# Output projection weights: split at the attention's end, or split on the way and kept in DRAM

## The chip, the cores and the metric

The kernel runs on one core of a Trainium2 chip. Its time is the device time of one launch in microseconds (us). Three runs of the kernel before took 2853.21, 2858.51 and 2867.74 us; the median is 2858.51. One further execution was taken with the hardware profiler; all views below are of that one.

## The reference, cut to what matters

Two transformer layers of width 1024 over 1024 prompt positions (one sequence) and 128 sample positions (8 streams of 16). Both groups go through the same layers, the sample group with cached keys and values.

```python
for l in range(2):
    sh_m, sc_m, g_m, sh_f, sc_f, g_f = split(silu(c) @ w_ada[l] + b_ada[l], 6)   # adaLN
    h = x * (1 + sc_m) + sh_m
    if l == 0:      # 16 query heads on 4 key/value heads of 64, own chunk of 64 + 2 back, sinks
        q, k, v = split(h @ w_qkv_a)
        o = band_attend(q, k, v, t5_bias, sinks, n_back=2);   mix = o @ w_o_a
    else:           # 16 heads, own chunk + 8 back; k, v projected once from x after layer 0
        q = h @ w_q_b
        o = band_attend(q, k_b, v_b, relclip_bias, None, n_back=8);  mix = o @ w_o_b
    x = layer_norm(ALPHA * x + (1 + g_m) * mix, ...)
    f = conv_ffn(x * (1 + sc_f) + sh_f, w_up[l], conv_w[l], conv_b[l], w_down[l])  # GEGLU, width 2816
    x = layer_norm(ALPHA * x + (1 + g_f) * f, ...)
# band_attend: s = q k^T * 64**-0.5 + bias, masked to the band; softmax (layer 0 with sink); p v
```

`o @ w_o_a` and `o @ w_o_b` are the output projections: 1024 x 1024 weights, 4 MB in fp32 each.

## The kernel before, in words

**High and low parts.** Wide products are made of fp32r matmuls on values split in two: a high part (the fp32 value cast to fp32r) and a low part (value minus high part). A product takes three matmuls: low by high, high by low, high by high. `split` (L174) does the cast on ACT (`copy`, L165) and the subtraction on POOL or DVE (L176). `wload` (L178) brings a piece of weights: SP issues the load of 128 x 1024 fp32 (512 KB) into `ws`, a staging ring of two buffers, and `split` writes its parts into a pair of buffers:

```python
s = (ring or self.ws).next()
self.nc.sync.dma_start(s, src)
h, l = dst or self.wring.next()
self.split(s, h, l, eh, el)
```

**Attention** (`attention`, L374). 16 heads (8 head pairs `c`, two heads `a` each) by 4 pairs of 128-row query tiles give 64 steps. A step issues, in this order: the scores of its pair (`scores`, L518: matmuls L546 with the high and L549 with the low part of the keys; bias, row minimum and exponential from L512 on), what the table `QAT` puts there of the query projection, the transposes of an earlier pair's probabilities (`weigh`, L557: matmul L572, high part L577 on ACT, low part L578 on DVE), and that pair's product with the values (`values`, L581: matmul L591, copy L602 on ACT, add L603 on DVE). After every second pair of a head, `normalise` (L621) multiplies by the reciprocal sums, which go to DRAM (rD) and come back spread over 64 rows (L628).

The query projection of head pair c is one `wload` (`qload`) and three blocks of 24 matmuls (`qblock`; the matmuls have line L302). Its weights go into `wslots[0:2]`, two slots, each a pair of `wh` and `wl` buffers of 128 x 1024:

```python
QAT[8 * c] = [(c + 1, None)]          # load weights of pair c + 1
self.wring = Ring(self.wslots[0:2])
```

The sample positions are 16 items, issued at the steps in `ITEMS` (matmuls and copies L672 to L735; one of them is the transpose L700). Layer 0's attention also carries the adaLN products of later use (`ada`, L237: matmuls of 32 x 256 with weights loaded into one buffer of `F`), a piece per step. Outputs `on` of head pairs 0 to 6 go to DRAM (`oN`) and are loaded and split into `H` at the steps in `OAT` (`oload`, L634); pair 7's are split from `on` itself.

During an attention, `wslots[2]` and half of `wslots[3]` hold split probabilities, the other half of `wslots[3]` holds keys, and `X1` (in the views `x1att`) holds keys, values and queries.

**Output projection** (`out_proj`, L921). Eight `wload`s bring the weights into eight pairs of buffers, all of them free again only as the attention ends: `wslots[0:2]`, parts of `X1`, `wslots[2]`. The first four are subtracted on POOL, the last four on DVE:

```python
w = [self.wload(wo[i // 4, i % 4], el="ppppvvvv"[i], dst=d) for i, d in enumerate(loc)]
```

`ln_gate` loads the gate row spread over 128 partitions into `gateP` = F[2048:3072]; `on` lies in F[2176:3200]. For each tile of 128 positions and half of the columns, `half` makes 24 matmuls (`mmX`, L314), multiplies by the gate (L948) and adds the residual (L949). Tile 8, the sample positions, comes third; its input is loaded from DRAM (`oSD`) and split (L966, L165, L176).

**What sets the order.** All transfers are issued by SP, one after the other. The program runs in a tile framework that orders each engine's instructions with its own model of time; instructions marked with `issue_after` follow a named one. Names in the views are of buffers (PS: the 8 banks of TensorE's results; HX: the buffer that holds `H`; C: small constants and sums; gatt: `rb`, `olo` and sample values of the attention).

Of the kernel before, what the change touches and what calls it, by code (L numbers as in the profile page):

```python
# [35 lines left out]
for c in range(5):  # L36
    QAT[8 * c] = [(c + 1, None)]
    for j, k in enumerate((1, 3, 6)):
        QAT[8 * c + k] = [(c + 1, j)]
QAT.update({40: [(6, None)], 41: [(6, 0)], 43: [(6, 1)], 46: [(6, 2)], 48: [(7, None), (7, 0)], 49: [(7, 1)], 50: [(7, 2)]})  # L40
OAT = {51: (0, 1), 52: (2,), 53: (3,), 54: (4,), 55: (5,), 61: (6,)}
ITEMS = [24 + 3 * k for k in range(8)] + [51 + (3 * k) // 2 for k in range(8)]
# [51 lines left out]
class Trunk:  # L94
    def __init__(self, ctx, tc, I, O):
# [4 lines left out]
        nc = self.nc  # L100
# [40 lines left out]
        self.vH = [dr.tile([1024, R[l] // 64, 128], F32, name=f"vH{l}") for l in range(2)]  # L141
        self.vS = [dr.tile([128, R[l]], F32, name=f"vS{l}") for l in range(2)]
        self.oN = dr.tile([7, 128, 1024], F32, name="oN")
        self.actD = dr.tile([NFF, 128, TOK], F32, name="actD")
# [229 lines left out]
    def attention(self, l, wk):  # L374
# [77 lines left out]

        self.wring = Ring(self.wslots[0:2])
        sbt = []
# [24 lines left out]
        def qblock(c, bi, w):  # L479
# [13 lines left out]
            for a in range(2):  # L493
                r = slice(64 * a, 64 * a + 64)
                o = slice(64 - 64 * a, 128 - 64 * a)
                hi = qs(c, a, r, s0, m)
                src = self.tiles(ps[r, 0:m])
                nc.scalar.activation(hi, src, AF.Copy, scale=-SCALE)
                nc.vector.scalar_tensor_tensor(
                    qs(c, a, o, s0, m), src, -SCALE, hi.bitcast(F32), op0=ALU.mult, op1=ALU.subtract  # L500
                )

        qw = {}
# [130 lines left out]
        def oload(c):  # L634
            s = self.ws.next()
            nc.sync.dma_start(s, self.oN[c])
            self.split(self.tiles(s), self.Hx(0, c, 0, 1024), self.Hx(1, c, 0, 1024), "a", "p")
# [130 lines left out]
        for i, x in enumerate(work):  # L768
# [19 lines left out]
            for c in OAT.get(i, ()):  # L788
                oload(c)
        assert not items  # L790
        for f in steps:
# [129 lines left out]
    def out_proj(self, l, xsrc, xdst, aff):  # L921
        nc, I, H = self.nc, self.I, self.H
        wo = I[("wo0", "wo1")[l]]
        X1 = self.X1
        loc = ((5120, 6144), (7168, 8192), (0, 2048), (3072, 1024))
        loc = [tuple(X1[:, o : o + 1024] for o in p) for p in loc]
        loc = self.wslots[0:2] + loc + [self.wslots[2], (X1[:, 4096:5120], self.wslots[3][1])]
        w = [self.wload(wo[i // 4, i % 4], el="ppppvvvv"[i], dst=d) for i, d in enumerate(loc)]
        w0, w1 = w[0:4], w[4:8]
        F = self.F  # L930
# [606 lines left out]
```

## Time and profile before

| what | value |
|---|---|
| runs | 2853.21, 2858.51, 2867.74 us, median 2858.51 |
| profiled execution | 2860.57 us, its span 2858.7 us |
| mean granted TensorE clock | 0.978 of full speed |
| PE busy | 2728.7 us, 95% of the span |
| DVE busy | 1675.0 us, 59% |
| ACT busy | 1404.6 us, 49% |
| POOL busy | 1078.0 us, 38% |
| transfers | 454.48 MB, mean 159 GB/s |

PE is TensorE's matmuls, PEld its weight loads, DVE VectorE, ACT ScalarE, POOL GpSimd, SP SyncE, which issues the transfers. A table by stretches gives for each the length, the busy time of PE, PEld, DVE, ACT and POOL with the number of instructions, the granted clock (1.00 is 2.4 GHz, 0.50 is 1.2 GHz), the mean busy share of the 16 DMA engines and what they moved in GB/s. A time line gives start, duration, engine, line, operation, output <- inputs, shape, and in brackets how long the engine had been idle and whose end it then started after. The scores of layer 0's attention begin at 112 us, those of layer 1's at 1589 us; the attentions end near 430 and 1975 us.

### The profile page before, as it was taken

The numbers are of one execution on the slowest core, as the hardware profiler recorded it, in microseconds if no ns is written. First come the engines' busy times: TensorE is split into PE (matmuls) and PEld (weight loads), VectorE is DVE, ScalarE is ACT, GpSimd is POOL, SyncE is SP. The second block draws the span as 40 slices with busy tenths as digits, with TensorE's granted clock in tenths as the row PEclk, the third lists the DMA queues.
The fourth block names the chain that finished last, engine by engine and source line by source line (L and its number), as shares of the span: only waits on it lengthen the run. The fifth ranks groups of instructions, "written<-read, shape, count | busy, mean of one in ns | idle before, by whom it ended". The sixth has DMA issues, their size and how long they took to land.

```text
span 2858.7 us, 48892 instructions
## 1 busy us (share of the span) xinstructions
PE 2728.7 (95%) x18086; PEld 2434.9 (85%) x18086; DVE 1675.0 (59%) x3841; ACT 1404.6 (49%) x2990; POOL 1078.0 (38%) x1104
## 2 busy tenths in 40 slices
PE   7999889899999999999999999988999999999998
PEld 4987767899999998788999888866799999997886
DVE  4365656765454556665412677774866555566764
ACT  3464643554444444445424676663465545554441
POOL 2122335776565640000550121231877666640000
PEclk9999989999999999999999999999999999999999
DMA  8655433244444448766785467683232222238662
GB/s 314 179 149 170 114 120 111 91 132 136 153 136 150 133 142 289 246 200 230 257 289 165 125 156 179 171 257 108 89 96 79 70 78 80 77 111 274 224 202 77
DMA packets 215199, 454.48 MB, mean 159 GB/s; under 512 B 38992, under 2 KB 114976, under 8 KB 214576
## 3 DMA queue, kind: packets, MB, share of 16 engines
q1 hardware_dynamic: 214960, 451.35, 49.7%
q8 instruction: 143, 2.34, 0.3%
q14 instruction: 96, 0.79, 0.1%
HBM read 359.40 MB, written 101.30 MB: 161 GB/s over the span
## 4 chain that ended last, share of the span: by engine, by line
PE 68%; issue 6%; DMA 4%; DVE 4%; ACT 2%; POOL 1%; SPq 0%; POOLq 0%; DVEq 0%; ACTq 0%
PE PS L1098 33%; PE PS L1249 15%; PE PS L302 7%; PE PS L314 7%; PE PS L591 1%; DMA ws<-in_wdn_dram 1%; PE PS L237 1%; PE PS L572 1%; DVE F L512 1%; PE PS L546 1%; PE PS L883 1%; DMA ws<-in_wo_dram 1%; PE PS L549 1%; DVE HX L176 0%; DMA F<-gd 0%
## 5 line engine op out<-in xcount | busy, mean ns | idle before, releaser
L176 POOL TENSOR_TENSOR wl<-ws,wh 128x512 fp32r<-128x512 f32 (+1 forms) x219 | 329.5, 1508 | 669.0 <-ACT wh L165 600.2
L1152 DVE SCALAR_TENSOR_TENSOR PS<-F,PS 128x512 f32<-128x512 f32 (+2 forms) x704 | 348.0, 515 | 141.0 <-ACT PS L1159 60.1
L1098 PE MATMUL PS<-HX,wh 128*128 128x288 f32 x2616 | 402.8, 298 | 14.1 <-DVE F L948 11.3
L165 ACT CAST wh<-ws 128x512 fp32r<-128x512 f32 (+1 forms) x321 | 244.9, 768 | 331.3 <-PE PS L1249 98.6
L1098 PEld LDWEIGHTS PS<-HX,wh 128*128 128x128 f32 x2616 | 366.0, 190 | 22.8 <-DVE F L948 11.7
L1249 PE MATMUL PS<-wh,HX 128*128 128x512 f32 x1164 | 364.6, 392 | 7.6 <-DVE HX L176 7.6
L1249 PEld LDWEIGHTS PS<-wh,HX 128*128 128x128 f32 x1164 | 219.5, 189 | 53.8 <-DVE HX L176 8.5
L1098 PE MATMUL PS<-HX,wl 128*128 128x288 f32 x1536 | 253.8, 296 | 1.0 <-DVE F L1134 0.7
L302 PE MATMUL PS<-HX,wh 128*128 128x384 f32 x1248 | 247.6, 340 | 0.0
L1249 PE MATMUL PS<-wl,HX 128*128 128x512 f32 x582 | 227.8, 391 | 0.6 <-DVE wl L176 0.6
L1098 PEld LDWEIGHTS PS<-HX,wl 128*128 128x128 f32 x1536 | 219.9, 188 | 7.6 <-issue 7.1
L302 PEld LDWEIGHTS PS<-HX,wh 128*128 128x128 f32 x1248 | 218.3, 190 | 4.6 <-issue 3.1
L314 PE MATMUL PS<-wh,HX 128*128 128x256 f32 (+1 forms) x936 | 173.7, 316 | 16.0 <-ACT wh L165 7.3
L1098 PE MATMUL PS<-x1att,wh 128*128 128x288 f32 x1168 | 182.2, 297 | 0.5 <-DVE x1att L176 0.5
L1159 ACT ACTIVATE PS<-F 128x512 f32<-128x512 f32 x176 | 138.2, 785 | 74.8 <-DVE F L1131 61.9
L165 ACT CAST HX<-F 128x384 fp32r<-128x384 f32 (+3 forms) x232 | 135.3, 602 | 75.5 <-PE PS L1249 15.6
L628 POOL TENSOR_TENSOR F<-F,gatt 64x512 f32<-64x512 f32 x62 | 79.4, 1281 | 243.9 <-DVE F L603 201.9
L176 DVE TENSOR_TENSOR HX<-F,HX 128x384 fp32r<-128x384 f32 (+3 forms) x204 | 147.2, 733 | 40.8 <-ACT HX L165 37.9
L1098 PEld LDWEIGHTS PS<-x1att,wh 128*128 128x128 f32 x1168 | 163.9, 188 | 5.9 <-issue 4.9
L314 PEld LDWEIGHTS PS<-wh,HX 128*128 128x128 f32 x936 | 137.5, 195 | 27.4 <-ACT wh L165 7.7
L1249 PE MATMUL PS<-HX 128*128 128x512 f32 x630 | 147.7, 394 | 4.5 <-ACT HX L165 4.5
L302 PE MATMUL PS<-HX,wl 128*128 128x384 f32 x624 | 133.4, 351 | 12.9 <-DVE HX L167 7.2
(242 smaller groups left out, 5515.4 us busy)
## 6 DMA issues: line engine op xcount, KB each, us to landing
F<-in_adaw_dram SPq DMA_DIRECT2D x106, 512.0 KB
ws<-in_wup_dram SPq DMA_DIRECT2D x92, 512.0 KB
ws<-in_wdn_dram SPq DMA_DIRECT2D x88, 512.0 KB
actD<-F SPq DMA_DIRECT2D x44, 576.0 KB
F<-actD SPq DMA_DIRECT2D x132, 192.0 KB
F<-in_wdn_dram SPq DMA_DIRECT2D x44, 512.0 KB
x1att<-kH SPq DMA_DIRECT2D x60, 256.0 KB
xd<-F SPq DMA_DIRECT2D x27, 512.0 KB
```

What stands on the lines that cost most here:

```text
L165: self.lastact = nc.scalar.copy(out, in_).ins
L176: self.eng(el).tensor_sub(lo, src, hi.bitcast(F32))
L237: mm = nc.tensor.matmul(ps[32 * j : 32 * j + 32, hf * 256 : hf * 256 + 256], self.cT[:, k * 32 : k * 32 + 32], w[n][:, j * 256 : j * 256 + ...
L302: self.nc.tensor.matmul(out, w[a][:, k * 128 : k * 128 + 128], self.Hx(p, k, s0, n), start=i == 0, stop=i == 23)
L314: self.nc.tensor.matmul(out[:, 0:n], H[:, t0 // 128, p, j * kn + k, :], w[a][:, k * n : k * n + n], start=i == 0, stop=i == 23,)
L512: nc.vector.tensor_tensor_reduce(out=p[:, c0 : c0 + w], in0=ps, in1=b, scale=1.0, scalar=init, op0=ALU.add, op1=ALU.min, accum_out=nm)
L546: mm = nc.tensor.matmul(o, q, khi[a][:, kc], start=first, stop=False, **kw)
L628: self.eng("v" if last else "p").tensor_mul(on[r, q], on[r, q], rb[r, :])
L1098: nc.tensor.matmul(out, w[f][a][:, k * 128 : k * 128 + 128], x[:, k, :], start=start and i == 0, stop=i == 11, skip_group_check=True,)
L1152: nc.vector.scalar_tensor_tensor(o, v, w(i), o, op0=ALU.mult, op1=ALU.add)
L1159: nc.scalar.activation(yp, u[:, bl, 2:258], AF.Identity, bias=w(3), scale=w(2))
L1249: nc.tensor.matmul(ps, h[p][:, i * 128 : i * 128 + 128], w[q][:, hf * 512 : hf * 512 + 512], start=j == 0 and k == 0, stop=j == NFF - 1 an ...
```

## The change

A new table, `WAT`, puts one function call at the end of steps 3, 9, 15, ..., 45 of each attention. The call, `wpre(i)`, does a `wload` of piece i of the output weights into `wslots[1]` (cast on ACT, subtraction on POOL) and stores both parts to `woD`, a new DRAM tensor. The query weights use `wslots[0]` alone. `out_proj` loads the 16 parts from `woD` into the same buffers as before and does no cast and no subtraction.

```diff
+WAT = {3 + 6 * i: i for i in range(8)}
...
+        self.woD = [dr.tile([8, 2, 128, 1024], F32, name=f"woD{l}") for l in range(2)]
...
-        self.wring = Ring(self.wslots[0:2])
+        self.wring = Ring(self.wslots[0:1])
...
+        def wpre(i):
+            w = self.wload(I[("wo0", "wo1")[l]][i // 4, i % 4], dst=self.wslots[1])
+            for p in range(2):
+                nc.sync.dma_start(self.woD[l][i, p], w[p].bitcast(F32))
...
             for c in OAT.get(i, ()):
                 oload(c)
+            if i in WAT:
+                wpre(WAT[i])
...
-        wo = I[("wo0", "wo1")[l]]
...
-        w = [self.wload(wo[i // 4, i % 4], el="ppppvvvv"[i], dst=d) for i, d in enumerate(loc)]
-        w0, w1 = w[0:4], w[4:8]
+        for i, d in enumerate(loc):
+            for p in range(2):
+                nc.sync.dma_start(d[p].bitcast(F32), self.woD[l][i, p])
+        w0, w1 = loc[0:4], loc[4:8]
```

The lines below a changed place move: L165, L176, L237 and L302 of before are L167, L178, L239 and L304 in the changed kernel, L546, L549, L572, L578, L591, L603 and L628 are L553, L556, L579, L585, L598, L610 and L635, and L948 is L958.

What stands on DVE at the end of layer 0's attention, from the last-but-one add L603 to the first product with the gate L948. L578 makes the last low parts of probabilities, `HX<-F,HX` of 128x1024 is the split of oSD, `HX<-F,HX` of 128x4x128 that of one half of pair 7's outputs, `wl<-ws` a split of output weights. Before:

```order
L176 TENSOR_TENSOR x1att_309<-ws,x1att_309 128x1024
L603 TENSOR_TENSOR F<-PS,gatt_310 64x256
L578 TENSOR_TENSOR wh<-PS,wh 128x512
L176 TENSOR_TENSOR HX<-F,HX 128x4x128
L176 TENSOR_TENSOR HX<-F,HX 128x1024
L603 TENSOR_TENSOR F<-PS,gatt_310 64x256 x2
L628 TENSOR_TENSOR F<-F,gatt_310 64x512
L176 TENSOR_TENSOR wl<-ws,wh 128x1024
L176 TENSOR_TENSOR wl<-ws,x1att_309 128x1024
L176 TENSOR_TENSOR HX<-F,HX 128x4x128
L948 TENSOR_TENSOR F<-PS,F 128x512 x2
```

The same place in the changed kernel:

```order
L610 TENSOR_TENSOR F<-PS,gatt_312 64x256
L585 TENSOR_TENSOR wh<-PS,wh 128x512
L610 TENSOR_TENSOR F<-PS,gatt_312 64x256
L178 TENSOR_TENSOR HX<-F,HX 128x4x128
L610 TENSOR_TENSOR F<-PS,gatt_312 64x256
L635 TENSOR_TENSOR F<-F,gatt_312 64x512
L178 TENSOR_TENSOR HX<-F,HX 128x1024
L178 TENSOR_TENSOR HX<-F,HX 128x4x128
L958 TENSOR_TENSOR F<-PS,F 128x512 x2
```

The subtractions of weights are gone, and the split of oSD stands behind the last adds and the last product with the reciprocal sums.

DVE at the end of layer 1's attention, with the same names. Before:

```order
L603 TENSOR_TENSOR F<-PS,gatt_12281 64x256
L578 TENSOR_TENSOR wh<-PS,wh 128x512
L578 TENSOR_TENSOR wh<-PS,wh 128x256
L176 TENSOR_TENSOR HX<-F,HX 128x1024
L176 TENSOR_TENSOR wl<-ws,wh 128x1024
L603 TENSOR_TENSOR F<-PS,gatt_12281 64x256
L176 TENSOR_TENSOR wl<-ws,x1att_12280 128x1024
L628 TENSOR_TENSOR F<-F,gatt_12281 64x512
L176 TENSOR_TENSOR HX<-F,HX 128x4x128
```

And in the changed kernel:

```order
L610 TENSOR_TENSOR F<-PS,gatt_12315 64x256
L585 TENSOR_TENSOR wh<-PS,wh 128x512
L178 TENSOR_TENSOR HX<-F,HX 128x1024
L585 TENSOR_TENSOR wh<-PS,wh 128x256
L610 TENSOR_TENSOR F<-PS,gatt_12315 64x256
L635 TENSOR_TENSOR F<-F,gatt_12315 64x512
L178 TENSOR_TENSOR HX<-F,HX 128x4x128
L958 TENSOR_TENSOR F<-PS,F 128x512 x2
```

Here the last low part of probabilities (128x256) stands behind the split of oSD instead of ahead of it.

PE at the start of layer 0's attention, where the projection of head pair 1 begins (L302, `PS<-HX,wl` first) behind that of pair 0. Before, with 4 attention matmuls and 4 of adaLN between the two projections:

```order
L302 MATMUL PS<-HX,wh 128x384 x16
L546 MATMUL PS<-x1att_309 128x128
L549 MATMUL PS<-x1att_309 128x128
L546 MATMUL PS<-x1att_309 128x256
L549 MATMUL PS<-x1att_309 128x256
L237 MATMUL PS<-F,C 32x256 x4
L302 MATMUL PS<-HX,wl 128x384 x8
```

In the changed kernel, the last rows of what stands between them:

```order
L579 MATMUL PS<-C,F 128x128 x2
L553 MATMUL PS<-x1att_311 128x256
L556 MATMUL PS<-x1att_311 128x256
L239 MATMUL PS<-F,C 32x256 x4
L553 MATMUL PS<-x1att_311 128x256
L556 MATMUL PS<-wl,x1att_311 128x256
L304 MATMUL PS<-HX,wl 128x384 x8
```

There the scores of more steps and the first transposes of probabilities (L579) come ahead of pair 1's projection, 19 score matmuls and transposes in all.

## Rows read from the trace of the kernel before

**Rows 1.** The page, busy us of each engine, share of the span, instructions.
```profile
PE 2728.7 (95%) x18086; PEld 2434.9 (85%) x18086; DVE 1675.0 (59%) x3841; ACT 1404.6 (49%) x2990; POOL 1078.0 (38%) x1104
```

**Rows 2.** Table by stretches, layer 0: us, engines, clock, DMA share, GB/s.
```profile
140.00:180.00 40.00, 39.67 (x296) 35.74 (x296) 26.38 (x90) 27.60 (x86) 10.74 (x14) 1.00 0.52 161
...
340.00:360.00 20.00, 14.31 (x99) 10.30 (x98) 13.09 (x56) 13.74 (x45) 8.62 (x9) 0.73 0.44 116
360.00:380.00 20.00, 18.12 (x130) 13.48 (x131) 13.29 (x52) 12.06 (x34) 9.73 (x6) 0.67 0.33 100
...
400.00:420.00 20.00, 17.72 (x104) 13.09 (x103) 7.04 (x17) 5.21 (x8) 6.64 (x4) 0.83 0.36 113
420.00:440.00 20.00, 13.10 (x45) 9.88 (x45) 8.68 (x12) 6.10 (x8) 3.82 (x3) 0.78 0.48 152
```

**Rows 3.** Table by stretches, layer 1.
```profile
1740.00:1780.00 40.00, 39.17 (x330) 33.49 (x330) 30.61 (x102) 27.05 (x70) 8.09 (x9) 1.00 0.80 213
...
1880.00:1900.00 20.00, 17.33 (x166) 13.38 (x164) 15.23 (x55) 11.72 (x30) 5.44 (x6) 0.97 1.02 286
```

**Rows 4.** Time line of ACT, end of layer 0: start, us, work, idle before.
```profile
406.75 1.05 ACT L165 CAST x1att<-ws 128x1024 fp32r<-128x1024 f32 x1 [5.13 <-DMA ws<-in_wo_dram]
...
413.76 1.05 ACT L165 CAST x1att<-ws 128x1024 fp32r<-128x1024 f32 x1 [4.96 <-DMA ws<-in_wo_dram]
...
422.23 1.04 ACT L165 CAST HX<-F 128x1024 fp32r<-128x1024 f32 x1 [3.64 <-DMA F<-oSD]
```

**Rows 5.** Time line of PE, end of layer 0.
```profile
409.96 0.44 PE L700 MATMUL PS<-C,F 128*128 128x128 f32 x2 [1.38 <-DVE HX L578]
...
425.03 1.54 PE L591 MATMUL PS<-wh,x1att 128*128 128x256 f32 x6 [2.94 <-DVE F L603]
427.98 2.08 PE L314 MATMUL PS<-wh,HX 128*128 128x512 f32 x4 [1.40 <-ACT wh L165]
```

**Rows 6.** Time line of DVE, end of layer 0.
```profile
427.46 0.69 DVE L628 TENSOR_TENSOR F<-F,gatt 64x512 f32<-64x512 f32 x1
428.19 1.23 DVE L176 TENSOR_TENSOR wl<-ws,wh 128x1024 fp32r<-128x1024 f32 x1
...
430.46 0.68 DVE L176 TENSOR_TENSOR HX<-F,HX 128x512 fp32r<-128x512 f32 x1
437.03 1.29 DVE L948 TENSOR_TENSOR F<-PS,F 128x512 f32<-128x512 f32 x2 [5.88 <-DMA F<-gd]
```

**Rows 7.** Time line of PE, end of layer 1.
```profile
1898.14 0.55 PE L572 MATMUL PS<-C,F 128*128 128x128 f32 x3 [1.97 <-DVE wh L578]
...
1909.22 1.02 PE L572 MATMUL PS<-C,F 128*128 128x128 f32 x6 [1.28 <-DVE wh L578]
...
1919.24 0.97 PE L572 MATMUL PS<-C,F 128*128 128x128 f32 x5 [1.35 <-DVE HX L578]
...
1932.34 0.72 PE L314 MATMUL PS<-wh,HX 128*128 128x512 f32 x2 [2.10 <-DVE C L512]
```

**Rows 8.** Time line of ACT, end of layer 1.
```profile
1867.24 1.05 ACT L165 CAST HX<-ws 128x1024 fp32r<-128x1024 f32 x1 [1.30 <-DMA ws<-oN]
...
1896.32 1.04 ACT L165 CAST wh<-ws 128x1024 fp32r<-128x1024 f32 x1 [2.72 <-DMA ws<-in_wo_dram]
```

**Rows 9.** Time line of DVE, end of layer 1.
```profile
1967.23 1.23 DVE L176 TENSOR_TENSOR wl<-ws,x1att 128x1024 fp32r<-128x1024 f32 x1
```

**Rows 10.** Time line of ACT, start of layer 0's attention.
```profile
113.81 1.04 ACT L165 CAST wh<-ws 128x1024 fp32r<-128x1024 f32 x1
```

**Rows 11.** Time line of POOL, start of layer 0's attention.
```profile
114.93 2.40 POOL L176 TENSOR_TENSOR wl<-ws,wh 128x1024 fp32r<-128x1024 f32 x1 [32.96 <-ACT wh L165]
```

**Rows 12.** Waits of PE, 100 to 340 us: total us, times, longest.
```profile
PE PS L237 <- DMA F<-in_adaw_dram: 5.8, 8, 2.7
```

**Rows 13.** The chain that ended last: start, us, what.
```profile
410.25 3.49 DMA ws<-in_wo_dram
...
1376.36 5.32 DMA hmD<-F
```

## The prediction

> **What bounds the kernel now.** I read the page's busy shares first, then the table by stretches over the two attentions, then the time lines of PE, ACT and DVE where the attentions end, then who waited for whom. PE is busy 95% of the span and no other engine over 59% [rows 1], so PE bounds it and a change is worth what it adds to or takes from PE's idle and slow time. In the middle of an attention there is next to none (39.67 of 40 us busy at a clock of 1.00, row 140:180 of [rows 2]), because the query projections (L302) fill PE between the scores. It lies at the end, where these are used up: PE is idle 5.7, 1.9, 2.3 and 6.9 us in the four 20 us stretches of layer 0's end that [rows 2] show, and the granted clock falls to 0.73, 0.67, 0.83 and 0.78. A granted clock c over a stretch of 20 us between the levels 1.2 and 2.4 GHz means (1 - c) * 2 * 20 us at the lower one: 10.8, 13.2, 6.8 and 8.8 us, 39.6 us together.
>
> The output weights sit in that end. The eight casts stand in ACT's queue among the copies that the attention needs, and ACT stood idle 5.13 and 4.96 us before two of them until their loads had landed [rows 4]. The attention's own copies (L577, L602) were behind. On PE this shows as 1.38 us (released by L578's result), 2.94 us (by L603) and 1.40 us (by a weight cast) of idle time [rows 5]. At the very end DVE's product with the gate (L948), for which PE's banks wait, waited 5.88 us for the gate row F<-gd [rows 6]. That row is loaded into the place of `on`, so it can't start before the last head is split.
>
> **The change part by part.** *End of layer 0.* All eight casts and eight subtractions leave it. The waits of [rows 4] that wait for in_wo go, and with them the 1.38 and the 1.40 us. The 2.94 us had another cause: ACT's cast of oSD, idle 3.64 us for its load [rows 4], stood ahead of the last-but-one copy L602, and DVE's subtraction ahead of L603. In the new order both last adds (now L610) stand before the oSD split, so this goes too: 5.72 us. After the last add the two weight subtractions on DVE ([rows 6], the first is shown, 1.23 us) no longer stand between the last product L628, which ended at 428.15, and the last split. That split's subtraction ran at 430.46; behind a cast of 0.62 us alone it could have run at 428.8, so the gate row starts 1.7 us earlier. Together -7.4 us. What is late next is the oSD chain itself: its load landed at 422.2, cast 1.04 and subtraction 1.22 us put the last split's subtraction at 424.5 and its end near 425.2, against 430.46 + 0.68 = 431.14 before, so even if no sample item comes earlier, 5.9 us are there. The far ends: -20 us, if PE's idle time of the end goes (12 of the 17 us of [rows 2]) and some 8 of the 39.6 us at the lower clock are won back; +3.6 us, if nothing is won and the gate row lands behind the two weight parts now queued before it, 512 KB each, at 1.8 us each (a stretch with the DMA engines full moved 286 GB/s, row 1880:1900 of [rows 3]).
>
> *End of layer 1.* Four gaps of PE stand behind ACT's queue in the same way, 1.97 + 1.28 + 1.35 + 2.10 = 6.7 us [rows 7]; before one cast ACT waited 2.72 us for in_wo [rows 8]. But casts of oN, which stay, wait for loads there too (1.30 us, [rows 8]), and the DMA engines are full from 1880 on [rows 3]. Sixteen loads of 512 KB stand where eight stood; some four of them fall into the full stretch, 4 * 1.8 = 7.3 us of transfer. At the last step two DVE subtractions go, one of which (1.23 us) ran between L603 and L628 [rows 9], but the last probability tile (L585, 128x256) now stands behind the oSD subtraction, so its products, copy and add come after it: about 2.4 us saved and 1.7 added. Between -7.5 and +7.3 us I take -2.5: a third of the gaps, since part of them stands behind oN.
>
> *One slot for query weights.* The cast of head pair 1 must now wait for the last matmul on pair 0's weights. In layer 0 it takes the place of the cast at 113.81 (1.04 us, [rows 10]), its low part is done at 114.93 + 2.40 = 117.33 [rows 11], and PE was busy with that pair's projection from 113.8. In the new order some 20 score matmuls and transposes stand before it instead. Between 0 and 3.5 us I take 1.5. At the later pairs 25 to 66 attention instructions of PE stand between two pairs' projections, where 19 to 69 stood, and cast and subtraction (3.4 us) lie beside them; in layer 1 pair 1's projection begins after 25 of them instead of 23, for which I take 0.5 us. Together +2, bounds 0 and 7.
>
> *The split during the attention.* Per layer 8 casts on ACT of 1.05 us, 8 subtractions on POOL of 2.4 us, 8 loads and 16 stores of 512 KB on SP. As many casts as before; four subtractions per layer move from DVE (1.23) to POOL, which is busy 10.74 of 40 us (140:180 of [rows 2]) and hides them. If that cover failed, 4 * 2.4 us a layer. The transfers are the open cost: 12 MB a layer, 43 us of full engines at 286 GB/s, in an attention where their share is 0.52 (layer 0, [rows 2]) and up to 0.80 (layer 1, [rows 3]). SP issues in order, so a store that waits for POOL holds what is queued behind it: bias rows for L512, rD and its way back for L628, and in layer 0 the adaLN weights, each loaded into one buffer that the matmul before must have left. PE waited for those 5.8 us in 8 of them, at most 2.7 [rows 12]. The lower bound is 0; the upper one transfer (1.8 us) on PE's path for each of 16 groups, 29 us. I take +3, nearer the lower, since 24 of the 32 adaLN loads cost PE nothing, and in layer 1 PE was busy 39.17 of 40 us beside a share of 0.80 (1740:1780 of [rows 3]).
>
> A store lands later than a load: 5.32 us against 3.49 [rows 13]. A group therefore needs 3.5 + 1.05 + 2.4 + 5.3 = 12.3 us before the slot is free, and the groups are six of 64 steps apart, about 29 us in an attention of some 311 us (113.81 in [rows 10] to 425.03 in [rows 5]), so the groups don't wait for each other. The Trainium skill (DMA: Bandwidth & Descriptors, section Anatomy of one DMA, SWDGE path) puts most of a transfer's fixed cost into the receipt of the write, worst where the target is HBM, which speaks against going through DRAM; by its fit for that path a 512 KB transfer takes an estimated 3.2 us. The trace agrees in kind, its store takes more, and with either the groups stay apart.
>
> **Sum.** -7.4 - 2.5 + 2 + 3 = -4.9 us against the profiled execution's 2860.6 us; that one is 2.1 us above the median of 2858.5, so 2853.5.
>
> **Rivals.** *Slower: SP's queue.* Each group puts one transfer of 1.8 us on PE's path, through the adaLN weights in layer 0 and the bias and key loads in layer 1. For it: the 5.8 us of [rows 12], a share of 0.80 in layer 1. Against: three quarters of those loads were hidden. The sum becomes -7.4 - 2.5 + 2 + 29 = +21, 2880. It decides from 0.5 us a group on (8 us eat the gain), and from 1.4 us a group the kernel is slower by 0.5%. *Faster: the ends run dense.* Both ends lose their waits and the clock stays up: -20 - 7.5 + 2 + 3 = -22.5, 2836. For it: 39.6 us at the lower clock in layer 0's end alone. Against: the oN loads before which ACT also waits, and the gate row, remain. The Trainium skill (TensorE: Matmul & The Clock Gate, section Why this matters for your kernels) says that idle gaps between bursts send the array back to half rate, so that a gap costs more than its length; the trace agrees (0.67 in 360:380 right behind the 5.7 idle us), and by that rule a removed gap, and an added one, counts double or more. *No gain:* the end is held by oSD and the gate row, the weight parts come no earlier than their places are free (keys and values until the last head), and only the 1.7 us are won: -1.7 + 0 + 2 + 3 = +3, 2862.
>
> **Chances.** Forecast 0.43, dense ends 0.22, SP's queue 0.20, no gain 0.15. About 0.5%, 14.3 us, is what a measurement can tell from no change. Faster by more: the dense ends and the forecast's edge, 0.26; slower by more: most of the queue case and an edge of the others, 0.20; within: 0.54. The likeliest case alone spans 2845 to 2862; the range, which takes in the dense ends and most of the queue case, 2836 to 2876.
>
> **What would show it.** Right: no ACT cast from ws<-in_wo near the ends; PE gaps before L598 and L579 there below 1 us; the first product with the gate (L958) 5 to 8 us earlier after layer 0's attention and 1 to 4 after layer 1's; a PE gap of 1 to 2 us before the first projection of pair 1; PE's wait for adaLN weights at most 8 us. Wrong: that wait at 15 us or more, SP long at the stores to woD, a clock below 0.9 in the middle of an attention, or the ends no shorter.

## The result, and the profile after

The changed kernel takes 2880.59 us (median of 5 runs, 2876.10 to 2882.50) against 2858.51: a ratio of 1.0076, 95% interval 1.0063 to 1.0089. It is slower by 22 us, where 5 us faster was forecast, and lies above the range. Its profiled execution took 2880.59 us with a span of 2878.8.

The page's busy times hardly move [rows 1]: PE 4.7 us more, and 20 us more span.

```profile
PE 2733.4 (95%) x18086; PEld 2440.0 (85%) x18086; DVE 1672.0 (58%) x3833; ACT 1404.4 (49%) x2990; POOL 1096.3 (38%) x1112
```

So 15 of the 20 us are time in which PE waits, and 5 are longer matmuls. The table by stretches of the changed kernel, layer 0 (columns as in [rows 2]):

```profile
140.00:180.00 40.00, 36.84 (x259) 32.18 (x260) 27.82 (x89) 28.65 (x84) 17.59 (x13) 0.96 0.74 248
...
360.00:380.00 20.00, 17.53 (x120) 12.67 (x121) 12.59 (x42) 8.84 (x27) 6.15 (x4) 0.54 0.27 80
...
420.00:440.00 20.00, 11.51 (x58) 8.57 (x59) 7.12 (x16) 5.26 (x8) 3.81 (x3) 0.75 0.66 177
```

The end still has idle time and a low clock, and the middle now has idle time. Layer 1 shows it better. From the first score matmul (on X1's high keys) to the 168th, layer 1 took 289.6 us before and takes 303.3 now: 13.7 us lost in one attention. Both stretches hold the same matmuls (2058 and 2059 in the rows). Before:

```profile
1588.90:1878.50 289.60, 279.03 (x2058) 246.89 (x2058) 208.71 (x671) 196.60 (x482) 62.62 (x63) 0.99 0.63 164
```

and in the changed kernel, which enters the attention some 11 us later:

```profile
1599.70:1903.00 303.30, 286.10 (x2059) 252.16 (x2058) 207.70 (x669) 201.65 (x487) 78.50 (x70) 0.97 0.71 205
```

PE is idle 17.2 us instead of 10.6, and busy 7.1 us longer with the same work, at a clock of 0.97 instead of 0.99. Two pieces of its first 60 us, each about as far behind the first score in both kernels. Before:

```profile
1589.00:1599.00 10.00, 8.63 (x52) 7.61 (x51) 5.58 (x22) 8.30 (x20) 2.36 (x1) 1.00 0.19 52
...
1639.00:1649.00 10.00, 9.82 (x64) 8.99 (x63) 7.43 (x25) 8.01 (x22) 1.29 (x1) 1.00 0.51 129
```

and now:

```profile
1600.00:1610.00 10.00, 6.05 (x25) 4.79 (x24) 5.00 (x21) 8.15 (x18) 4.67 (x2) 0.71 0.58 201
...
1650.00:1660.00 10.00, 7.26 (x38) 6.43 (x37) 5.67 (x20) 7.06 (x17) 2.36 (x1) 0.83 0.56 191
```

The time line of the changed kernel there, by engines, says how:

```profile
1595.91 0.33 SPq L508 DMA_DIRECT2D woD<-wl  x1
1596.34 0.44 SPq L182 DMA_DIRECT2D ws<-in_wo_dram  x1
...
1601.70 1.04 ACT L167 CAST wh<-ws 128x1024 fp32r<-128x1024 f32 x1 [4.38 <-DMA ws<-in_wo_dram]
1602.76 0.56 ACT L489 ACTIVATE F<-PS 64x128 f32<-64x128 f32 x2
1603.33 0.38 ACT L500 ACTIVATE x1att<-PS 64x256 fp32r<-64x256 f32 x1
...
1603.74 0.42 DVE L501 SCALAR_TENSOR_TENSOR x1att<-PS,x1att 64x256 fp32r<-64x256 f32 x1 [2.94 <-ACT x1att L500]
1604.19 0.69 DVE L519 CUSTOM_DVE_ANT_0 F<-PS,F 128x512 f32<-128x512 f32 x1
...
1604.94 0.64 PE L553 MATMUL PS<-x1att 128*128 128x320 f32 x1 [3.24 <-DVE C L519]
```

Read upwards from PE. It waits 3.24 us for a bank that DVE's softmax step has to empty. DVE stood before L501, which needs ACT's copy of the queries, L500. ACT stood 4.38 us before a weight cast, whose load had been issued only at 1596.34, right behind the store of the piece before. PE's next instruction is the score matmul that needs the bank, so PE stands still. Over both attentions (the view of the tile in_wo: who waited for its loads) ACT stood 29.8 us ahead of 12 of the 16 casts:

```profile
  ACT wh L167: 29.8, 12
```

At the ends the forecast waits are gone, but others stand in their place. End of layer 0 (against [rows 5, 6]):

```profile
426.69 0.39 SPq L938 DMA_DIRECT2D wh<-woD  x1
427.11 0.43 SPq L938 DMA_DIRECT2D x1att<-woD  x1
433.30 0.32 SPq L836 DMA_DIRECT2D F<-gd  x1
...
436.83 1.22 PE L316 MATMUL PS<-wh,HX 128*128 128x512 f32 x2 [6.03 <-DMA wh<-woD]
...
430.72 0.69 DVE L635 TENSOR_TENSOR F<-F,gatt 64x512 f32<-64x512 f32 x1 [3.54 <-DMA gatt<-rD]
...
439.38 1.29 DVE L958 TENSOR_TENSOR F<-PS,F 128x512 f32<-128x512 f32 x2 [6.11 <-DMA F<-gd]
```

The last weight parts can be loaded only when the last probabilities have left `wslots[2]`, and PE then waits 6.03 us for a whole transfer, which ends some 10 us after its issue (426.69, 436.83). Before, the raw piece lay in `ws` by then, and only a cast and a subtraction were left. The gate row's load was issued at this point before:

```profile
431.18 0.33 SPq L827 DMA_DIRECT2D F<-gd  x1
```

End of layer 1 (against [rows 7 to 9]):

```profile
1985.96 1.04 ACT L167 CAST HX<-F 128x1024 fp32r<-128x1024 f32 x1 [5.69 <-DMA F<-oSD]
1986.91 0.36 ACT L584 CAST wh<-PS 128x256 fp32r<-128x256 f32 x1
...
1987.04 1.23 DVE L178 TENSOR_TENSOR HX<-F,HX 128x1024 fp32r<-128x1024 f32 x1 [6.04 <-ACT HX L167]
1988.18 0.42 DVE L585 TENSOR_TENSOR wh<-PS,wh 128x256 fp32r<-128x256 f32 x1
...
1988.65 1.12 PE L598 MATMUL PS<-wh,x1att 128*128 128x128 f32 x4 [6.22 <-DVE wh L585]
```

The split of oSD, which is needed only for the third tile, waits for its load ahead of the last probabilities.

### The profile page after: what moved, and what is told of

It is laid out like the page before. It is cut to its first block, busy times and chain, and to the rows that moved or that the text cites. A ratio compares the mean times of both kernels' runs of the same rounds, so it can differ in the third digit from the quotient of the medians.

```text
span 2878.8 us, 49031 instructions
## 1 busy us (share of the span) xinstructions
PE 2733.4 (95%) x18086; PEld 2440.0 (85%) x18086; DVE 1672.0 (58%) x3833; ACT 1404.4 (49%) x2990; POOL 1096.3 (38%) x1112
## 5 line engine op out<-in xcount | busy, mean ns | idle before, releaser
L178 POOL TENSOR_TENSOR wl<-ws,wh 128x512 fp32r<-128x512 f32 (+1 forms) x231 | 357.5, 1551 | 691.3 <-ACT wh L167 612.3
L167 ACT CAST wh<-ws 128x512 fp32r<-128x512 f32 (+1 forms) x331 | 255.3, 776 | 351.1 <-PE PS L1259 96.0
L1108 PE MATMUL PS<-HX,wh 128*128 128x288 f32 x2616 | 402.8, 298 | 13.7 <-DVE F L958 10.9
L1108 PEld LDWEIGHTS PS<-HX,wh 128*128 128x128 f32 x2616 | 366.0, 190 | 22.4 <-DVE F L958 11.4
L304 PE MATMUL PS<-HX,wh 128*128 128x384 f32 x1248 | 247.4, 343 | 0.0
L304 PEld LDWEIGHTS PS<-HX,wh 128*128 128x128 f32 x1248 | 221.2, 192 | 4.9 <-issue 3.5
L167 ACT CAST HX<-F 128x384 fp32r<-128x384 f32 (+3 forms) x232 | 135.5, 602 | 80.9 <-PE PS L1259 14.2
L178 DVE TENSOR_TENSOR HX<-F,HX 128x384 fp32r<-128x384 f32 (+3 forms) x204 | 147.6, 736 | 37.5 <-ACT HX L167 33.7
L635 POOL TENSOR_TENSOR F<-F,gatt 64x512 f32<-64x512 f32 x62 | 79.4, 1281 | 197.7 <-DVE F L610 137.7
L304 PE MATMUL PS<-HX,wl 128*128 128x384 f32 x624 | 134.8, 354 | 13.6 <-DVE HX L169 7.7
```

The costliest lines, as they stand in the source:

```text
L167: self.lastact = nc.scalar.copy(out, in_).ins
L178: self.eng(el).tensor_sub(lo, src, hi.bitcast(F32))
L304: self.nc.tensor.matmul(out, w[a][:, k * 128 : k * 128 + 128], self.Hx(p, k, s0, n), start=i == 0, stop=i == 23)
L635: self.eng("v" if last else "p").tensor_mul(on[r, q], on[r, q], rb[r, :])
L1108: nc.tensor.matmul(out, w[f][a][:, k * 128 : k * 128 + 128], x[:, k, :], start=start and i == 0, stop=i == 11, skip_group_check=True,)
```

## The experiments

Each kernel was timed beside the kernel before on the same chip; differences are of the medians of one such pair (before: 2856.75, 2856.14, 2858.69, 2858.23, 2856.85 us).

| kernel | median us | minus before | ratio, 95% | layer 1, first to 168th score |
|---|---|---|---|---|
| one_slot | 2865.28 | +8.5 | 1.0016 to 1.0035 | 288.6 |
| two_direct | 2851.00 | -5.8 | 0.9973 to 0.9993 | 289.8 |
| one_direct | 2856.25 | -0.5 | 0.9985 to 1.0004 | 287.9 |
| pre_oldend | 2885.00 | +28.3 | 1.0086 to 1.0114 | 303.4 |
| transfers_only | 2868.82 | +12.7 | 1.0034 to 1.0065 | 289.4 |
| split_no_load | 2872.55 | +16.4 | 1.0046 to 1.0079 | 298.6 |
| pool_cast | 2868.03 | +11.9 | 1.0024 to 1.0055 | 294.8 |
| pinned | 2869.74 | +13.6 | 1.0037 to 1.0063 | 301.0 |
| late_osd_pool | 2868.07 | +9.4 | 1.0026 to 1.0057 | 293.5 |
| two_early | 2865.50 | +6.8 | 1.0014 to 1.0040 | 295.0 |
| late_osd_before | 2848.39 | -10.3 | 0.9957 to 0.9981 | 287.8 |
| late_osd_poolend | 2851.64 | -7.1 | 0.9970 to 0.9991 | |
| only0_act | 2874.64 | +16.4 | 1.0038 to 1.0077 | 289.7 |
| only1_act | 2865.97 | +7.7 | 1.0018 to 1.0043 | 299.8 |
| only0_pool | 2872.73 | +14.5 | 1.0037 to 1.0077 | 289.9 |
| only1_pool | 2854.65 | -3.6 | 0.9982 to 1.0006 | 293.9 |
| few_before | 2864.97 | +8.1 | 1.0018 to 1.0037 | |
| few_only0_pool | 2864.75 | +7.9 | 1.0014 to 1.0036 | |

**The change in its parts.** One slot alone:

```diff
-        self.wring = Ring(self.wslots[0:2])
+        self.wring = Ring(self.wslots[0:1])
```

> The kernel before with one slot for the query weights and nothing else. Between the first score and the 3/4 point of the scores, the changed kernel lost 8 us in layer 0 and 13.7 us in layer 1, and won some of it back at the ends. If the one slot makes this loss (head pair c+1 can't be cast until pair c's last projection, so PE has no filler between the scores), this kernel takes 2870 to 2882 us and shows PE waiting for DVE's softmax and a fallen clock in the first 60 us of each attention. If the split and its 24 MB of transfers make the loss, it takes 2858 to 2863 us.

The end alone, with two slots:

```diff
-        w = [self.wload(wo[i // 4, i % 4], el="ppppvvvv"[i], dst=d) for i, d in enumerate(loc)]
+        for d in loc:
+            for p in range(2):
+                nc.sync.dma_start(d[p].bitcast(F32), self.woD[l])
...
         qload(0)
+        nc.sync.dma_start(self.woD[l], qw[0][0].bitcast(F32))
```

> The kernel before with two query slots and no split at all: out_proj loads its 16 parts from one DRAM tile of 512 KB that is stored once per layer, so the output projection's weights are wrong and their loads and splits are left out. It prices the end alone. Both theories: the attention up to its 3/4 point as before, the ends 7 to 12 us shorter, 2846 to 2853 us. If 16 loads of 512 KB at the end cost as much as the splits did, 2858 or more.

The same with one slot:

> As the one before (one DRAM tile, no splits, wrong weights), with one query slot: the changed kernel without its splits and stores in the attention. If the one slot makes the loss, 2866 to 2878 us, within 10 us of the changed kernel, with the same idle time at the attentions' starts. If the transfers and splits make it, 2846 to 2856 us.

And the changed kernel's attention with the end of before (`out_proj` as it was):

> The changed kernel's attention (one slot, splits, stores) with the output projection of before (8 loads, casts and subtractions at the end; woD is written and never read). If the ends of the changed kernel won 7 to 12 us, this one is that much slower than it: 2887 to 2893 us. If the 16 loads gave the win back, the same 2880 us.

Both theories as first put were too simple. One slot costs 8.5 us with the old end and 5.3 with the new one, by the profiles nearly all of it in layer 0: layer 1's first score comes 6.7 us later than before in one_slot (1595.6 against 1588.9) and 5.0 us later in one_direct than in two_direct (1592.1 against 1587.1), and layer 1's stretch is 288.6 and 287.9 us, no longer than before. The end gives 5.8 us with two slots. The rest comes with the split in the attention: 2885.00 - 2865.28 = 19.7 us with the old end, and about 23 with the new one (the changed kernel's +22.1 against one_direct's -0.5). Only kernels that split on the way lose layer 1's 14 us (303.3, 303.4).

**What of the split costs.** Loads and stores without casts and subtractions:

```diff
-            w = self.wload(I[("wo0", "wo1")[l]][i // 4, i % 4], dst=self.wslots[1])
+            nc.sync.dma_start(self.ws.next(), I[("wo0", "wo1")[l]][i // 4, i % 4])
+            w = self.wslots[1]
+            self.step(self.bgrate)
```

> The changed kernel without the casts and subtractions of the output weights: the 16 loads from in_wo and the 32 stores to woD stay (the stores take what stands in the slot, so these weights are wrong), and so do the loads at the end. In the changed kernel's trace ACT stood idle 29.8 us ahead of 12 of the 16 casts until their loads had landed. If that wait, with the copies and exponentials queued behind it, makes the 20 us between the kernels with and without the split in the attention, this one takes 2855 to 2862 us. If the transfers themselves make it (full engines, loads for PE held in SP's queue), 2873 to 2882.

Casts and subtractions without loads:

```diff
-            w = self.wload(I[("wo0", "wo1")[l]][i // 4, i % 4], dst=self.wslots[1])
+            w = self.wslots[1]
+            self.split(self.H[:, 0, 0].rearrange("p c n -> p (c n)").bitcast(F32), *w, "a", "p")
+            self.step(self.bgrate)
```

> The changed kernel with casts, subtractions and stores, but without the 16 loads from in_wo: the split reads a part of the layer's input that lies in place, so these weights are wrong. No cast has a load to wait for; ACT and POOL do the same work, and the stores still wait for POOL in SP's queue. If ACT's wait for the loads makes the loss, 2857 to 2866 us. If the work of the split on ACT and POOL or the stores make it, 2874 to 2882.

The casts on POOL:

```diff
-            w = self.wload(I[("wo0", "wo1")[l]][i // 4, i % 4], dst=self.wslots[1])
+            w = self.wload(I[("wo0", "wo1")[l]][i // 4, i % 4], eh="p", dst=self.wslots[1])
```

> The changed kernel with the casts of the output weights on POOL instead of ACT. POOL then waits for the loads, and the copies of queries and the exponentials on ACT have nothing of the output weights ahead of them. If ACT's wait makes the loss, 2858 to 2870 us (POOL's own queue, with the fill of the bias and the products L635, may be late by some us). If transfers or SP's queue make it, 2878 to 2884.

The order written out:

```diff
+        wsq, wso = Ring(self.ws.items[0:1]), self.ws.items[1]
...
+        def wpre(i):
+            with self.tc.issue_after(self.lastexp):
+                self.split(wso, *self.wslots[1], "a", "p")
+        def wput(i):          # three steps later
+            with self.tc.issue_after(self.lastbias):
+                for p in range(2):
+                    nc.sync.dma_start(self.woD[l][i, p], self.wslots[1][p].bitcast(F32))
+                if i < 7:
+                    wnext(i + 1)      # load of the next piece into wso
```

> The changed kernel with another order of the same work: the load of piece i+1 is issued behind the bias load three steps ahead of its cast, into a staging buffer of its own (query weights use the other one), the cast stands behind the exponentials of its step, and the stores of a piece are issued three steps after its split. If ACT's wait for the loads makes the loss, it falls below 5 us in sum here, and the kernel takes 2856 to 2866 us. If the transfers make it, 2874 to 2882.

Three of the four medians lie between what the theories gave, and pool_cast's 2868.03 near the upper edge of what ACT's wait alone would leave (2858 to 2870), so neither is the whole. Layer by layer they are clearer. Without casts layer 1's loss is gone with all transfers in place (289.4). In layer 0 the same transfers raise PE's waits for adaLN weights. The waits of PE from 112 to 340 us, without the split (one_direct):

```profile
PE PS L238 <- DMA F<-in_adaw_dram: 5.7, 6, 1.4
```

and with transfers alone:

```profile
PE PS L239 <- DMA F<-in_adaw_dram: 15.2, 11, 5.2
```

In the changed kernel they were 7.8 us. So this kernel, in which nothing holds a store back, overstates them. In split_no_load no cast has a load to wait for, and layer 1 stays long all the same (298.6). Its eight casts of output weights there start within 49 us (1581.70 to 1630.26) and wait for POOL twice, 0.82 and 1.54 us; the waits for stores (11.3 us in 3 casts) all stand in layer 0. So a load isn't needed for a loss: casts that crowd the attention's start are enough, though this kernel doesn't separate them from their subtractions and stores, which crowd with them. In pinned ACT waits for no output weights, and their loads stand apart as the program spaces them, 26 to 37 us. The first 220 us from layer 1's first score, before, in pinned, with the casts on POOL (only1_pool, below), in split_no_load, and with the change in layer 1 as it was (only1_act, below):

```profile
1588.90:1808.90 220.00, 212.98 (x1546) 189.69 (x1546) 160.63 (x515) 149.41 (x371) 42.61 (x46) 1.00 0.61 156
1592.90:1812.90 220.00, 213.14 (x1538) 188.62 (x1538) 158.79 (x510) 155.03 (x376) 58.36 (x52) 1.00 0.72 201
1590.90:1810.90 220.00, 213.55 (x1548) 189.99 (x1548) 159.80 (x515) 149.44 (x371) 65.32 (x59) 1.00 0.74 206
1599.20:1819.20 220.00, 210.28 (x1497) 187.53 (x1499) 154.27 (x491) 149.18 (x363) 55.80 (x51) 0.98 0.65 183
1584.80:1804.80 220.00, 208.49 (x1475) 183.52 (x1474) 151.74 (x485) 149.00 (x362) 57.56 (x52) 0.98 0.70 202
```

PE does 1546 matmuls before, 1538 in pinned and 1475 in only1_act. Seven of pinned's eight casts lie in these 220 us, so casts of 1.05 us on ACT cost layer 1 next to nothing when they stand apart and find their data there. Pinned loses its 11.4 us later: a load of oN, issued among loads of keys and values, holds a cast on ACT for 6.91 us, and the same jam comes back from another load. Its SP, ACT and PE:

```profile
1872.91 0.54 SPq L654 DMA_DIRECT2D ws<-oN  x1
...
1881.76 1.04 ACT L167 CAST HX<-ws 128x1024 fp32r<-128x1024 f32 x1 [6.91 <-DMA ws<-oN]
1882.71 0.58 ACT L595 CAST wl<-PS 128x512 fp32r<-128x512 f32 x1
...
1884.07 0.37 PE L634 MATMUL PS<-C 128*4 128x128 f32 x1 [6.84 <-DVE wl L596]
```

**By layers.** In these four kernels `WAT`, the one slot and the loads from woD hold for one layer, and the other is as before:

```diff
-            if i in WAT:
+            if i in WAT and l == 1:
```

> The whole change in layer 0, layer 1 as before. In the changed kernel's profile layer 0 with its feed-forward part took 10.6 us more than before. If it is a cost of layer 0's attention itself (loads for PE late in SP's queue, late projection of pair 1), 2866 to 2871 us; if the two layers' costs only arise together or that number is scatter of one execution, below 2863.

> The whole change in layer 1, layer 0 as before. In the changed kernel's profile the stretch from the first score of layer 1 to its 3/4 point lost 13.7 us, with ACT waiting 15.9 us for loads of output weights, and the rest of the program won 4.2 back: 2865 to 2871 us expected by that. If layer 0 makes the loss, 2853 to 2859.

> The change in layer 0 alone, with the weight casts on POOL. ACT's wait is gone there too. If ACT's wait makes layer 0's loss as well, 2855 to 2860 us. If the one slot and the loads for PE (adaLN weights) make it, 2862 to 2868, close to the kernel with the casts on ACT.

> The change in layer 1 alone, with the weight casts on POOL. If ACT's wait makes all of layer 1's loss, only the gain of the end is left: 2851 to 2857 us, 10 or more below the kernel with the casts on ACT. If transfers or the one slot make part of it, 2860 or more.

This settles most of layer 1. The only edit between only1_act and only1_pool is the engine of the cast, and it is worth 11.3 us: with the casts on ACT the change costs 7.7, without them it wins 3.6 (an interval that reaches to no change). The edit takes both the casts and their wait (13.6 us in layer 1 of only1_act) out of ACT's queue; pinned, whose casts stay on ACT, says that the wait counts and not the casts' own work. Of the stretch, 4.3 us stay lost (293.9 against 289.6), all of them behind the first 220 us, where PE waited 2.66 us for cached values and 3.21 us behind a cast of oN; whether the new transfers delay these loads isn't tested. Layer 0 costs 16.4 and 14.5, whoever casts, both more than the dearer case that was expected. The layers add up: 16.4 + 7.7 = 24.1 against 22.1, 14.5 - 3.6 = 10.9 against pool_cast's 11.9.

**Layer 0.** In `ada` all loads but the first of a group are left out:

```diff
-                nc.sync.dma_start(w[n], self.I["adaw"][gi, n // 2, n % 2])
+                if n == 0 or gi not in (1, 2):
+                    nc.sync.dma_start(w[n], self.I["adaw"][gi, n // 2, n % 2])
```

> The kernel before with 2 instead of 32 loads of adaLN weights in layer 0's attention (the first piece of each group is used for all 16, so these products are wrong; the matmuls stay). PE waited 5.8 us for these loads in all: 2850 to 2856 us. It is the base for the next kernel.

> The change in layer 0 alone with the casts on POOL, again with 2 instead of 32 loads of adaLN weights. With all 32 this change cost 14.5 us. If the output weights' transfers cost PE time through the adaLN loads in SP's queue, the change costs 8 us or less without these loads (2858 to 2864 against the kernel before with few loads at 2853); if the one slot and the order make it, it still costs 12 us or more (2865 to 2869).

By the letter the second came out as the transfers theory said: the change costs nothing (2864.75 against 2864.97). But its base missed: with 30 loads fewer the kernel before is 8.1 us slower. The adaLN matmuls of it and of the kernel before (minimum, median and longest in ns, first and last start):

```profile
L238 PE MATMUL PS<-F,C x256: 379/379/636, 115.7 to 199.2; 128*32 128x256 f32 x128
```

```profile
L237 PE MATMUL PS<-F,C x256: 379/403/636, 113.3 to 309.0; 128*32 128x256 f32 x128
```

Without the loads to pace them they are over at 199 us instead of 309. That the attention's second half then lacks work to fill PE's gaps is argued, not shown. The pair therefore doesn't separate the loads from the order. Of layer 0's 14.5 us, one slot makes 5.3 to 8.5; the rest stays open.

The profiles say where in layer 0 it lies, though single executions of the same layer 0 differ by several us. From the first to the last score matmul of layer 0 the kernels with two slots, no split and all adaLN loads took 270.5 to 277.7 us (before 277.0), one_slot and one_direct 287.3 and 283.0, the changed kernel 286.4, and only0_act 294.6. So one slot alone reaches what the changed kernel loses in this attention, and the split can add to it.

**The ends.**

```diff
-                self.split(s3, H[:, t, 0], H[:, t, 1], "a", "v")
+                with self.tc.issue_after(self.lastcopy), self.tc.issue_after(self.lastadd):
+                    self.split(s3, H[:, t, 0], H[:, t, 1], "a", "v")
```

with `lastcopy` and `lastadd` the copy (L602) and add (L603) of the attention's last step. On pool_cast:

> The kernel with the weight casts on POOL, and with the split of oSD issued on ACT and DVE behind the attention's last copy and last add. In the changed kernel at the end of layer 1 PE waited 6.22 us for the last low part of probabilities, which stood on DVE behind the split of oSD, whose load ACT awaited for 5.69 us. If that order makes the 6.2 us, the last products come 4 to 6 us earlier: 2861 to 2865 us against 2868. If the gate row or the last weight parts, which the first products need as well, end at the same time, 2866 to 2870.

The wait of 6.2 us went, and another took its place, as the second half of the expectation has it. PE of this kernel:

```profile
1968.82 0.66 PE L598 MATMUL PS<-wh,x1att 128*128 128x128 f32 x4
1974.03 1.98 PE L316 MATMUL PS<-wh,HX 128*128 128x512 f32 x4 [4.55 <-DMA wh<-woD]
```

The median is the same 2868 us, +9.4 against its own base where pool_cast had +11.9. Then two slots for the first pairs, pieces from step 9 on:

```diff
-WAT = {3 + 6 * i: i for i in range(8)}
+WAT = {9 + 5 * i: i for i in range(8)}
...
-        self.wring = Ring(self.wslots[0:1])
+        self.wring = Ring([self.wslots[i] for i in (0, 1, 0, 0, 0, 0, 0, 0)])
```

> As the one before, with two slots for the query weights at the start: head pair 1 uses the second slot, and the pieces of the output weights come into it from step 9 on, five steps apart. The kernel before with one slot and nothing else was 8.5 us slower. If that price is paid at the start of the attention, where pair 1 can't be cast while pair 0 is projected, this kernel is 5 to 9 us faster than the one with one slot: 2854 to 2860 us. If it is paid all along, the difference is below 3 us.

2.6 us less, with intervals that overlap: below the 5 to 9 that the slot was to give back at the start, and so the expectation's other case, that its price is paid all along. And the late split of oSD in the kernel before, alone:

> The kernel before, with the split of oSD behind the attention's last copy and add, and nothing else. Its ends hold the eight weight casts as well, so the gain is smaller than in the changed kernel: 2851 to 2857 us against 2856.5; in the trace the wait of PE for the last weight cast at the end of layer 1 (5.5 us) stays if the casts hold it, and goes below 2 us if oSD did.

and with casts and subtractions of the last four pieces on POOL:

> The one before with the casts of the last four output weight pieces, and their subtractions, on POOL instead of ACT and DVE. It tests whether the gain of the changed kernel's ends (5.8 us without any splits there) can be had by keeping the casts out of ACT's queue, with no store to DRAM: 2847 to 2854 us if so. If POOL's chain (cast, then 2.4 us of subtraction for each piece) is later than ACT's and DVE's, 2857 to 2864.

The first beats both kernels by more than expected: -10.3 us, ratio 0.9969 (0.9957 to 0.9981). Before, the same jam stood at layer 1's end. ACT and PE of the kernel before:

```profile
1963.32 1.04 ACT L165 CAST HX<-F 128x1024 fp32r<-128x1024 f32 x1 [4.67 <-DMA F<-oSD]
1964.27 1.04 ACT L165 CAST wh<-ws 128x1024 fp32r<-128x1024 f32 x1
...
1965.36 2.08 PE L314 MATMUL PS<-wh,HX 128*128 128x512 f32 x4 [5.54 <-ACT wh L165]
```

and with the late split:

```profile
1952.50 1.05 ACT L165 CAST wh<-ws 128x1024 fp32r<-128x1024 f32 x1
...
1957.19 1.57 ACT L165 CAST HX<-F 128x1024 fp32r<-128x1024 f32 x2 [2.29 <-DMA F<-oSD]
...
1953.61 1.21 PE L314 MATMUL PS<-wh,HX 128*128 128x512 f32 x4
...
1964.26 1.29 DVE L948 TENSOR_TENSOR F<-PS,F 128x512 f32<-128x512 f32 x2 [4.16 <-DMA F<-gd]
```

The weight cast that PE waited 5.54 us for had its data; it stood behind the split of oSD. What ends last now is the gate row. From layer 1's last score to the first product with the gate (L948) it takes 47.7 us instead of 54.0, and the kernels with the same end there 52.9 to 53.8; where the other 4 us come from isn't shown. Moving weight casts to POOL as well loses 3 us of this by the medians (the intervals overlap), though it lies in the range that its expectation gave for a gain.

## Why the prediction was wrong

**The step that failed** is in the split during the attention: "the groups are six of 64 steps apart, about 29 us in an attention of some 311 us, so the groups don't wait for each other". Six steps is where the program writes them. In layer 1 of the changed kernel the loads of the first six pieces were issued within 83 us, the first two of them 10 us apart, and four of the five later ones directly behind the stores of the piece before, which wait for POOL. The first and the sixth:

```profile
1586.51 0.50 SPq L182 DMA_DIRECT2D ws<-in_wo_dram  x1
...
1669.83 1.05 SPq L182 DMA_DIRECT2D ws<-in_wo_dram  x1
```

So a load comes late, and its cast holds ACT. For that the sum had no term: of ACT it says "As many casts as before". ACT's wait for in_wo, which the prediction counted as removed with the waits of [rows 4, 8], moved along with the casts to places where more stood behind it (23.0 us in 9 casts before, 29.8 in 12 now). Where the loads do stand apart (pinned), the first 220 us of the attention are as dense as before.

**The term.** "I take +3, nearer the lower" measured 20 to 23 us, inside its bounds of 0 and 29 and near the upper one. The mechanism priced there, transfers on PE's path through SP's queue, was not the main one where the cause is settled: layer 1's part is the casts that wait in ACT's queue, 11.3 us by only1_act and only1_pool. PE's waits for adaLN weights were 7.8 us, within the 8 that the prediction allowed. That the rival "SP's queue" gave 2880 is a coincidence of size in layer 1; in layer 0, where 14.5 us stay without ACT's wait, it may hold a part.

**One slot**, +2 with bounds 0 and 7, measured 8.5 (5.3 with the new end). Layer 1's 0.5 was right in size (its stretch did not grow). The cost lies in layer 0, whose attention took 10.3 us longer in one_slot (287.3 against 277.0), and not in a gap ahead of pair 1's projection; that the later projection moves the filler is argued, not shown.

**The ends**, -7.4 and -2.5, measured -5.8 together without any split. The direction was right, and the profiles say where the rest went. From the attention's last score to the first product with the gate the changed kernel takes 39.1 us in layer 0 and 49.7 in layer 1; pre_oldend, which has the same attention and the old end, takes 46.0 and 52.9. So 6.9 and 3.2 us are won there, close to the forecast, and in part by luck, since the waits of 6.03 and 6.22 us that stand there now were not foreseen. But from that product to layer 1's first score the changed kernel takes 1160.3 us against 1152.0. All profiled kernels with direct loads at layer 0's end take 1154.4 to 1160.5 us for it, and before, one_slot, pre_oldend, only1_act and only1_pool 1151.6 to 1154.3. A part of layer 0's win, in the changed kernel all of it, is given back in a stretch for which the prediction has no term; by what, isn't tested.

On the clock of the execution the gate row of layer 0 landed 2.3 us later than before (439.38 against 437.03, after 1.2 us of later start and with the last score 10.6 us later). The reason that the far end gave, the weight parts queued before it, is not what the rows show: from its issue to the product it took 6.1 us (from 433.30), and 5.9 before (from 431.18). It was the issue that came later, and on DVE the product L635, which stands ahead of the last split, had waited 3.54 us for the sums on their way back from rD. In layer 1 the moved L585 was seen, and priced at 1.7 us; it was 6.22, since the oSD cast ahead of it waited for its load.

**The signs named** came out so: no in_wo cast near the ends, right; gaps before L598 and L579 below 1 us, wrong in layer 1 (6.22 and 1.40; layer 0's last ones are 0.98 and 0.63); a gap of 1 to 2 us before pair 1's first projection, wrong, none stands there; PE's wait for adaLN weights at most 8 us, right; the first product with the gate earlier, wrong on the clock of the execution, right in size against pre_oldend's end (6.9 and 3.2 us). Of the signs against, SP stood ahead of its stores to woD for 20.0 us in layer 0 and 13.7 in layer 1. A clock below 0.9 in the attention is there, in its first 60 us and not in its middle: 0.71 from 1600 to 1610 and 0.83 from 1650 to 1660, where before had 1.00. PE's two longest waits in that attention, 3.24 and 2.57 us, stand in these two pieces. That agrees with the rule of the Trainium skill ("TensorE: Matmul & The Clock Gate", section Why this matters for your kernels) that idle gaps send the array back to half rate. A gap then costs more than its length: of the 13.7 us, 6.6 are more idle time and 7.1 longer matmuls.

## What to carry to other kernels

A step that is moved takes its wait with it: before counting a wait as removed, see where the waiting instruction stands afterwards, and what is queued behind it there. Where a scheduler places work, spacing in the program is no spacing on the queues; read how far each load stands ahead of its first user. And when a wait ends with an engine's result, look one instruction up in that engine's queue: the cast that seemed to wait for weights waited behind a split that nobody needed yet, and moving that won 10.3 us, twice what the change was forecast to win.

## What was not expected of the hardware

Taking away 30 loads of 512 KB made the kernel 8.1 us slower (few_before). These loads had spread the short matmuls behind them (256 in the view) over 196 us; that this is the reason isn't shown. And a load straight into place can be the later one where the place becomes free late: with the last weight parts loaded directly PE waited 6.03 us (4.55 in late_osd_pool), while a cast of 1.05 and a subtraction of 1.23 us stood there before. Over the whole end the direct loads were the shorter way even so (two_direct, -5.8).
